# The input norm of a hybrid encoder block: token by token from a token-major copy, instead of raw projections that are scaled afterwards

## The chip, the cores and the metric

The kernel runs on one core of one Trainium2 chip. The metric is the device time of one execution in microseconds (us). The core has five engines that run side by side: PE (TensorE, matmuls; its weight loads are listed as PEld), DVE (VectorE), ACT (ScalarE), POOL (GpSimd) and SP (SyncE, which here only issues transfers). Work passes between them by semaphores.

## The reference, cut to what matters

One layer: an RMS norm, one wide projection `w_in`, three token mixers whose results are gated and merged, an output projection, and an MLP. What the change touches is the first norm and the first users of its result:

```python
def rms_norm(x, g):
    y = x * lax.rsqrt(jnp.mean(x * x, axis=-1, keepdims=True) + EPS)
    return y * g

h = rms_norm(x, norm1_g)                  # x: 512 tokens x 1024 features
p = h @ w_in                              # N_IN = 3*1024 + 2*1024 + 3*1024 + 3*1024+256 columns
pa, pb, pg, pc = _split(p, ...)
pc = token_shift(pc, rwkv_mu)             # p + (previous token's p - p) * mu
r, k, v, xw, xa, xg = _split(pc, ...)     # 1024, 1024, 1024, 64, 64, 128 columns
decay = exp(-exp(-softplus(-(w0 + tanh(xw) @ w2)) - 0.5))
a = sigmoid(a0 + xa @ a2);  g_c = sigmoid(xg) @ g2
# short convolution, RG-LRU, RWKV-7 recurrence over chunks of 64 tokens, merge with gates
x = x + m @ w_out
x = x + square(relu(rms_norm(x, norm2_g) @ mlp_w1)) @ mlp_w2
return rms_norm(x, final_g)
```

All of it is float32. The norm's factor belongs to a token, so it commutes with a projection: `(x * g) @ w` can be formed first and its row multiplied by the token's root afterwards.

## The kernel before, in words

**Layout.** Activations stand feature-major: 128 features on the partitions, the 512 tokens (`S`) along the row, eight such tiles (`KT`) for 1024 features. A projection of 128 columns (a "chunk") takes eight 128x128 weight tiles. To keep float32 accuracy each operand is split into a rounded high half and a remainder, `whi`/`wlo` for a weight and `hh`/`hl` for the normed input, and `mm3` (L168 to L171) issues three matmuls for each tile, so a chunk is 24 matmuls of 128x512. A weight is loaded on SP's queue into one of two `raw` buffers, ACT casts the high half (L148), and DVE subtracts for the low half (L105); three buffers of each half rotate.

**The start.** SP loads x feature-major (`xT`, from `xt`) in five pieces, with halves of the first two weights between them. For each of the eight tiles ACT forms `xgh` (x times the norm's gain, rounded) and the square, DVE the remainder `xgl` and the sum of two squares, and PE adds the squares over the features by a matmul with a tile of ones into `pst`. PE projects from `xgh` and `xgl` at once, before the root is known: chunk `lr 0`, later `lr 1`, `k 0` and `r 0` (`proj_raw`; these are the raw projections). `rsqrt_rows` makes the root on DVE by two transposes and three Newton steps. Then `pro_scale` multiplies `xT` by the root and makes `hh` and `hl`, which all further chunks use, and `unscaled` multiplies the four raw results by the root.

**The order.** A scheduler orders each engine's queue by priority. Generators are woven: `krv(g)` prepares the keys, values and receptance of head group g (`pw`, `pa`, `pn`, `pb`, `pV` are its small matmuls), `amat(g)` the matrices within chunks (`pA`, masked by DVE into `AXt`, then transposes `pB`), `inverse` inverts them, `chain` is the recurrence; the steps of `ab(q)` and `gate(q)`, projections of the other two mixers and of the gates, fill in between. `weave(krv(0), fl, R0)` takes 0.85 fill steps for each step of `krv(0)`. In `krv` the first k and r were not projected, since `k0` and `r0` existed.

**POOL.** It issues the transfers through DRAM that rearrange heads and chunks. `ttd` is a DRAM buffer of which one part is zeroed from a tile `zer`; `in_eyes` is a table of identities for `inverse`, loaded into a tile that shares its buffer (tag Z) with half of `xgh`.

Of the kernel before, what the change touches and what calls it, by code (L numbers as in the profile page):

```python
# [99 lines left out]
def block_kernel(ctx, tc, xt, win, par, mulr, sw, wout, w1, w2, fg, cst, eyes, out):  # L100
# [3 lines left out]
    def tt(o, a, b, op):  # L104
        return v.tensor_tensor(out=o, in0=a, in1=b, op=op)  # L105

    def stt(o, a, s, b, op0, op1):
        return v.scalar_tensor_tensor(out=o, in0=a, scalar=s, in1=b, op0=op0, op1=op1)  # L108
# [59 lines left out]
    def mm3(ps, wh, wl, xh, xl, start=True, stop=True):  # L168
        pe.matmul(ps, wh, xh, start=start, stop=False)  # L169
        pe.matmul(ps, wh, xl, start=False, stop=False)  # L170
        pe.matmul(ps, wl, xh, start=False, stop=stop)  # L171
# [71 lines left out]
    wlr = [new_w()]
    load_half(wlr[0], win[CN[("lr", 0)]], 0)
    for a, n in ((0, 1), (1, 1), (2, 2)):
        sy.dma_start(xT[:, a:a + n], xt[a:a + n].rearrange("k p t -> p k t"))
    load_half(wlr[0], win[CN[("lr", 0)]], 1)
    for a, n in ((4, 2), (6, 2)):
        sy.dma_start(xT[:, a:a + n], xt[a:a + n].rearrange("k p t -> p k t"))
    wlr.append(new_w())  # L250
    for i in range(2):
        load_half(wlr[1], win[CN[("lr", 1)]], i)
    gp.memset(epst[:, 0:1], EPS)
# [1 line left out]
    gp.memset(one, 1.0)
    wu = pc.tile([P, S], F32, tag="pu", name="wu")
    for i in range(NWARM):
        pe.matmul(wu, ones, zer, start=True, stop=True)
    pst = pm.tile([P, S], F32, tag="pm", name="pst")
    warm = pro.tile([P, 1], F32, name="warm")  # L260
    ac.activation(warm, epst[:, 0:1], AF.Tanh)

    t_lr0 = pp.tile([P, S], F32, tag="pp", name="pp")
    sqp_ctx = ExitStack()
    sqp = sqp_ctx.enter_context(tc.tile_pool(name="sqp", bufs=1))
    for kt in range(KT):
        sq = (p1 if kt % 2 else sqp).tile([P, S], F32, tag=f"v{kt // 2 % 2}" if kt % 2 else f"sq{kt // 2}", name="sq")
        ac.activation(xgh(kt), xT[:, kt], AF.Copy, scale=n1t[:, kt:kt + 1])
        stt(xgl[:, kt], xT[:, kt], n1t[:, kt:kt + 1], f(xgh(kt)), MUL, SUB)
        with tc.high_priority(offset=OFFP):  # L270
            ac.activation(sq, xT[:, kt], AF.Square)
            if kt % 2 == 1:
                tt(sq, sq, sq_, ADD)
                pe.matmul(pst, ones, sq, start=kt == 1, stop=kt == KT - 1)
        mm3(t_lr0, *wslice(wlr[0], kt), xgh(kt), xgl[:, kt], start=kt == 0, stop=kt == KT - 1)
        sq_ = sq
# [6 lines left out]
    sy.dma_start(ident, cst[:, 0:P])  # L283
    sy.dma_start(mask, cst[:, 2 * P:3 * P])

    def pro_scale():
        for kt in range(KT):
            tt(xT[:, kt], xT[:, kt], rsb, MUL)
            ac.activation(hh[:, kt], xT[:, kt], AF.Copy, scale=n1t[:, kt:kt + 1])
            stt(hl[:, kt], xT[:, kt], n1t[:, kt:kt + 1], f(hh[:, kt]), MUL, SUB)  # L290
        ac.copy(bd, c0)

    def proj_raw(w, t):
        for kt in range(KT):
            mm3(t, *wslice(w, kt), xgh(kt), xgl[:, kt], start=kt == 0, stop=kt == KT - 1)
# [64 lines left out]
    shift(unscaled(t_lr0, "us0"), mul[:, 0:1], omul[:, 0:1], lr)  # L360
    t_k0 = pp.tile([P, S], F32, tag="pp", name="pp")
    proj_raw(load_w(win[CN[("k", 0)]]), t_k0)
    t_r0 = pc.tile([P, S], F32, tag="pS", name="r0")
    proj_raw(load_w(win[CN[("r", 0)]]), t_r0)
# [57 lines left out]
    def krv(g, G_):  # L422
# [3 lines left out]
        for jj in range(2):  # L426
            j = 2 * g + jj
            if j == 0:
                ks, rs = k0, r0
            else:  # L430
                ks, rs = WP("ks"), WP("rs")
                t = yield from proj(("k", j))
                shift(t, pv("mu_k", j), dvp(OMK, j), ks)
# [882 lines left out]
```

## Time and profile before

| | us |
|---|---|
| median of 3 runs | 1028.8 |
| lowest, highest | 1027.36, 1030.81 |
| the profiled execution | 1029.49 |
| its span on the core | 1027.7 |

| engine | busy us | share of the span |
|---|---|---|
| PE | 1007.2 | 98% |
| PEld | 817.7 | 80% |
| DVE | 735.1 | 72% |
| ACT | 512.9 | 50% |
| POOL | 110.1 | 11% |

The profile is one execution, recorded by the hardware. The span runs from the first instruction of the program to the last; what lies around it is the difference to the execution's time, 1.8 us. A row of the order of time has the start, the length, the engine, the line in the kernel, the operation, what it writes and reads, its shape and how many were merged, and in brackets the idle time of the engine before it and what ended it. PE's matmuls are pipelined: their lengths overlap, so the distance of two starts tells what one costs.

### The profile page before, as it was taken

To read this page: it belongs to the slowest core of one execution; us is meant where nothing else is said; L and a number is where in the kernel's file an instruction comes from. 1 tells how busy PE (TensorE), PEld (TensorE's weight loads), DVE (VectorE), ACT (ScalarE), POOL (GpSimd) and SP (SyncE) were. 2 spreads that over 40 slices of the span, in tenths; PEclk is the share of its full clock that TensorE was granted. 3 is DMA by queue.
4 is the path that set the end of the run, shared out by engine and by line. 5 is a ranking of instruction groups with operands and counts; after the bars stand their busy time and mean duration, and the time that the engine had idled before them with its cause. 6 is when DMAs were issued, how large, how long until landed. Compare 5 with 4: busy or idle time off the path is not lost. (4 is left out here: it accounts for less than half of the span.)

```text
span 1027.7 us, 15699 instructions
## 1 busy us (share of the span) xinstructions
PE 1007.2 (98%) x6110; PEld 817.7 (80%) x6110; DVE 735.1 (72%) x1251; ACT 512.9 (50%) x757; POOL 110.1 (11%) x179
## 2 busy tenths in 40 slices
PE   8999999999999999999999999999999999999997
PEld 5777877888887788888787877888888888878885
DVE  6997497599865886794668779656554546887775
ACT  7756453655554655456446344435433334454344
POOL 1013011201212112001322100100000000000001
PEclk9999999999999999999999999999999999999999
DMA  6444643734546446434897724544333325644442
GB/s 231 129 123 112 185 134 114 215 107 128 150 134 164 136 126 161 158 95 122 268 256 243 220 87 119 174 132 130 90 99 103 98 87 164 226 127 139 143 166 102
DMA packets 49177, 151.53 MB, mean 147 GB/s; under 512 B 6544, under 2 KB 10128, under 8 KB 48080
## 3 DMA queue, kind: packets, MB, share of 16 engines
q1 hardware_dynamic: 34816, 99.93, 30.6%
q0 software_dynamic: 13568, 49.56, 18.0%
q8 instruction: 48, 0.79, 0.3%
q10 hardware_dynamic: 720, 1.05, 0.3%
q14 instruction: 25, 0.20, 0.1%
HBM read 123.78 MB, written 26.74 MB: 146 GB/s over the span
## 5 line engine op out<-in xcount | busy, mean ns | idle before, releaser
L148 ACT CAST whi<-raw 128x1024 fp32r<-128x1024 f32 (+1 forms) x164 | 169.7, 1037 | 257.0 <-PE pp L170 86.7
L105 DVE TENSOR_TENSOR wlo<-raw,whi 128x1024 fp32r<-128x1024 f32 (+1 forms) x176 | 206.5, 1175 | 91.2 <-ACT whi L148 90.6
L169 PE MATMUL pp<-hh,whi 128*128 128x512 f32 x688 | 271.2, 395 | 0.4 <-DVE rs L108 0.4
L170 PE MATMUL pp<-hl,whi 128*128 128x512 f32 x688 | 270.1, 393 | 0.0
L171 PE MATMUL pp<-hh,wlo 128*128 128x512 f32 x688 | 269.1, 391 | 0.2 <-DVE wlo L105 0.2
L169 PEld LDWEIGHTS pp<-hh,whi 128*128 128x128 f32 x688 | 129.1, 188 | 28.9 <-DVE rs L108 0.9
L171 PEld LDWEIGHTS pp<-hh,wlo 128*128 128x128 f32 x688 | 129.2, 188 | 27.5 <-DVE wlo L105 0.6
L170 PEld LDWEIGHTS pp<-hl,whi 128*128 128x128 f32 x688 | 129.2, 188 | 26.3
L169 PE MATMUL p<-h2h,whi 128*128 128x512 f32 x256 | 100.4, 392 | 0.0
L171 PE MATMUL p<-h2h,wlo 128*128 128x512 f32 x256 | 99.7, 389 | 0.0
L170 PE MATMUL p<-h2l,whi 128*128 128x512 f32 x256 | 99.6, 389 | 0.0
L108 DVE SCALAR_TENSOR_TENSOR r<-p,rsb 128x512 f32<-128x512 f32 x32 | 22.0, 691 | 69.3 <-PE p L171 68.8
L171 PEld LDWEIGHTS p<-h2h,wlo 128*128 128x128 f32 x256 | 48.1, 188 | 10.2
L169 PEld LDWEIGHTS p<-h2h,whi 128*128 128x128 f32 x256 | 48.1, 188 | 9.8
L170 PEld LDWEIGHTS p<-h2l,whi 128*128 128x128 f32 x256 | 48.1, 188 | 9.6
L1225 POOL TENSOR_TENSOR x0f<-xr,fgt 128x512 f32<-128x512 f32 x4 | 5.2, 1296 | 310.6 <-DMA raw<-in_w 301.4
L170 PE MATMUL acc<-ml,whi 128*128 128x512 f32 x64 | 25.0, 391 | 0.0
L171 PE MATMUL acc<-mh,wlo 128*128 128x512 f32 x64 | 25.0, 390 | 0.0
L1076 PE MATMUL acc<-whi,a2h 128*128 128x512 f32 x64 | 24.9, 389 | 0.0
L1076 PE MATMUL acc<-whi,a2l 128*128 128x512 f32 x64 | 24.9, 389 | 0.0
L1076 PE MATMUL acc<-wlo,a2h 128*128 128x512 f32 x64 | 24.9, 389 | 0.0
L1076 PE MATMUL acc<-whi,ah 128*128 128x512 f32 x64 | 24.9, 389 | 0.0
(368 smaller groups left out, 1733.5 us busy)
## 6 DMA issues: line engine op xcount, KB each, us to landing
raw<-in_win SPq DMA_DIRECT2D x88, 512.0 KB, 3.6
raw<-in_w SPq DMA_DIRECT2D x64, 512.0 KB, 3.6
ax<-axd POOLq DMA_DIRECT2D x8, 1024.0 KB, 10.0
axd<-AXt POOLq DMA_DIRECT2D x12, 512.0 KB, 8.7
raw<-in_w SPq DMA_DIRECT2D x24, 256.0 KB, 2.9
bkd<-BKT POOLq DMA_DIRECT2D x4, 1024.0 KB, 15.4
raw<-in_wout SPq DMA_DIRECT2D x8, 512.0 KB, 3.6
bk<-bkd POOLq DMA_DIRECT2D x7, 512.0 KB, 13.0
```

The costliest lines, as they stand in the source:

```text
L105: return v.tensor_tensor(out=o, in0=a, in1=b, op=op)
L108: return v.scalar_tensor_tensor(out=o, in0=a, scalar=s, in1=b, op0=op0, op1=op1)
L148: ac.copy(hi[:, sl], raw[:, sl])
L169: pe.matmul(ps, wh, xh, start=start, stop=False)
L170: pe.matmul(ps, wh, xl, start=False, stop=False)
L171: pe.matmul(ps, wl, xh, start=False, stop=stop)
L1076: pe.matmul(b[i], x_[:, ms], w_, start=id(b[i]) not in begun, stop=last and n == 2, skip_group_check=True)
L1225: gp.tensor_tensor(out=o0, in0=x0, in1=fgt[0], op=MUL)
```

## The change

x comes a second time, as `xn`: four tiles of 128 tokens with all 1024 features in the row, loaded into `xs` at the head of SP's queue. The feature-major copy is no longer loaded here. For each token tile ACT squares the row and accumulates it to one number per token, ACT takes a root, DVE corrects its reciprocal by one Newton step, and multiplies an identity by it to a diagonal `dg`. PE multiplies each 128x128 tile of `xs` by the diagonal (`turn`), which transposes it to feature-major and scales each token at once, into PSUM banks `tb`; there are 32 such turns. From `tb` ACT and DVE make `hh` and `hl`. All projections now use these, so `proj_raw`, `pro_scale`, `unscaled`, `xgh`, `xgl` and the matmuls over squares are gone. Both `lr` chunks are projected side by side; `k 0` and `r 0` become ordinary steps of `krv(0)`. Ahead of the first turn stand matmuls of ones with ones that keep PE occupied (`warm`, 12 and three after each of the first three tiles). The zeros for `ttd` come from a small tile made later, and a root taken early on ACT before the end's norm is gone.

```diff
-NWARM = 2
+NWARM, NFILL = 12, 3
...
-    xT = p1.tile([P, KT, S], F32, tag="AXt", name="xT")
-    xgh_ = [p1.tile([P, 4, S], F32R, tag=t, name="xgh") for t in ("BKT", "Z")]
+    xs = p1.tile([P, 4, D], F32, tag="AXt", name="xs")
...
+    ac.dma_start(ident, cst[:, 0:P])
     ac.dma_start(n1t, par[:, PI["n1"]])
+    with tc.high_priority(offset=1000):
+        for i in range(3):
+            sy.dma_start(xs[:, i], xn[i])
+        for h in range(2):
+            sy.dma_start(xs[:, 3, h * S:(h + 1) * S], xn[3, :, h * S:(h + 1) * S])
...
+    def warm(n):
+        for i in range(n):
+            pe.matmul(wu[:, 0:P], ones, ones, start=True, stop=True)
+    warm(NWARM)
...
+    def turn(kt, i):
+        pe.matmul(tb[kt][:, i * P:(i + 1) * P], xs[:, i, kt * P:(kt + 1) * P], dg[:, i], start=True, stop=True)
+
+    with tc.high_priority(offset=1000):
+        for i in range(4):
+            if i < 3:
+                ac.activation(junk, xs[:, i], AF.Square, accum_out=ssq[:, 0, i:i + 1])
+            else:
+                for h in range(2):
+                    ac.activation(junk[:, h * S:(h + 1) * S], xs[:, 3, h * S:(h + 1) * S], AF.Square,
+                                  accum_out=ssq[:, h, 3:4])
+                tt(ssq[:, 0, 3:4], ssq[:, 0, 3:4], ssq[:, 1, 3:4], ADD)
+            ac.activation(ssq[:, 1, i:i + 1], ssq[:, 0, i:i + 1], AF.Sqrt, bias=epst[:, 0:1], scale=1.0 / D)
+            m_, y_ = ssq[:, 0, i:i + 1], ssq[:, 1, i:i + 1]
+            v.reciprocal(y_, y_)
+            ts2(m_, m_, -0.5 / D, -0.5 * EPS, MUL, ADD)
+            stt(m_, m_, y_, y_, MUL, MUL)
+            stt(m_, m_, 1.5, y_, ADD, MUL)
+            v.tensor_scalar(out=dg[:, i], in0=ident, scalar1=ssq[:, 0, i:i + 1], scalar2=None, op0=MUL)
+            if i < 3:
+                for kt in range(5):
+                    turn(kt, i)
+                warm(NFILL)
+
+    wlr = [load_w(win[CN[("lr", i)]]) for i in range(2)]
...
+    def normed(kt):
...
+        for i in range(3 if kt < 5 else 0, 4):
+            turn(kt, i)
+        ac.activation(hh[:, kt], tb[kt], AF.Copy, scale=n1t[:, kt:kt + 1])
+        stt(hl[:, kt], tb[kt], n1t[:, kt:kt + 1], f(hh[:, kt]), MUL, SUB)
...
+        for kt in range(KT):
+            if kt and kt + 4 < KT:
+                normed(kt + 4)
+            for w, t in zip(wlr, t_lr):
+                mm3(t, *wslice(w, kt), hh[:, kt], hl[:, kt], start=kt == 0, stop=kt == KT - 1)
...
-    def pro_scale():
-        for kt in range(KT):
-            tt(xT[:, kt], xT[:, kt], rsb, MUL)
...
-    def unscaled(t, tag):
...
-            if j == 0:
-                ks, rs = k0, r0
-            else:
...
+            ks, rs = WP("ks"), WP("rs")
+            t = yield from proj(("k", j))
...
-        gp.dma_start(ttd[32:64, g, :, 0:32], zer[0:32, 0:32].unsqueeze(1).to_broadcast([32, NC * 4, 32]))
+        gp.dma_start(ttd[32:64, g, :, 0:32], zz.unsqueeze(1).to_broadcast([32, NC * 4, 32]))
...
-        ac.activation(epst, epst, AF.Sqrt)
-        gp.memset(epst, EPS)
```

How the queues change at the places that matter. First PE at the start of the program, before (`wu` is the bank of the warming matmuls, `pst` the sum of squares, `pp` a projection's bank):

```order
L258 MATMUL wu<-zer,ones 128x512 x2
L274 MATMUL pst<-sq,ones 128x512
L169 MATMUL pp<-xgh,whi 128x512
L170 MATMUL pp<-xgl,whi 128x512
L171 MATMUL pp<-xgh,wlo 128x512
L169 MATMUL pp<-xgh,whi 128x512
L274 MATMUL pst<-sq,ones 128x512
```

And PE now, from the last token tile's turns on (`tb_124` to `tb_249` are the eight feature tiles, `pp_200` is lr 0 and `pp_201` lr 1):

```order
L262 MATMUL tb_128<-dg_131,xs_97 128x128
L169 MATMUL pp_200<-hh_73,whi_189 128x512
L170 MATMUL pp_200<-hl_74,whi_189 128x512
L171 MATMUL pp_200<-hh_73,wlo_190 128x512
L262 MATMUL tb_223<-dg_131,xs_97 128x128 x4
L169 MATMUL pp_200<-hh_73,whi_189 128x512
L170 MATMUL pp_200<-hl_74,whi_189 128x512
L171 MATMUL pp_200<-hh_73,wlo_190 128x512
L169 MATMUL pp_200<-hh_73,whi_189 128x512
L169 MATMUL pp_201<-hh_73,whi_195 128x512
```

The first projection, which came behind one matmul over two tiles' squares, now comes behind the turns of all four token tiles. Next ACT at the same place, now:

```order
L270 ACTIVATE junk_129,ssq_130<-xs_97 128x512 x2
L273 ACTIVATE ssq_130<-ssq_130,epst_68 128x1
L148 CAST whi_189<-raw_188 128x1024
L294 ACTIVATE hh_73<-tb_124,n1t_101 128x512
L294 ACTIVATE hh_73<-tb_125,n1t_101 128x512
L294 ACTIVATE hh_73<-tb_126,n1t_101 128x512
L294 ACTIVATE hh_73<-tb_127,n1t_101 128x512
L294 ACTIVATE hh_73<-tb_128,n1t_101 128x512
L148 CAST whi_195<-raw_194 128x1024
L294 ACTIVATE hh_73<-tb_223,n1t_101 128x512
```

The first weight's cast stands ahead of the first `hh`, the second weight's cast between the fifth and the sixth. Last, POOL at the start, before:

```order
L308 MEMSET smk 128x512
L874 DMA ttd<-zer 32x32x32
L309 MEMSET smk 128x8
L874 DMA ttd<-zer 32x32x32 x3
L463 MEMSET PPt 128x8
L1057 MEMSET epst 128x1
L562 DMA Z<-in_eyes 128x1024
L489 DMA rtd<-AR 128x8x64
```

and now:

```order
L323 MEMSET smk 128x512
L555 DMA Z<-in_eyes 128x1024
L324 MEMSET smk 128x8
L482 DMA rtd<-AR 128x8x64
L456 MEMSET PPt 128x8
```

The zeros of `ttd` have left the start, and the load of the identities for `inverse`, whose buffer is no longer held by raw x, has come forward to it.

More of the change, by code (lines that the diff above doesn't have):

```diff
@@ L99, in block_kernel @@
 @with_exitstack
-def block_kernel(ctx, tc, xt, win, par, mulr, sw, wout, w1, w2, fg, cst, eyes, out):
+def block_kernel(ctx, tc, xt, win, par, mulr, sw, wout, w1, w2, fg, cst, eyes, xn, out):
     nc = tc.nc
@@ L239, in block_kernel @@
-    gp.memset(zer, 0.0)
     gp.memset(ones, 1.0)
+    gp.memset(epst[:, 0:1], EPS)
     n1t = pro.tile([P, KT], F32, name="n1t")
+    ac.dma_start(ident, cst[:, 0:P])
     ac.dma_start(n1t, par[:, PI["n1"]])
[L243 to L253, printed above, removed]
+    with tc.high_priority(offset=1000):
[3 more added lines that the diff above has]
+            sy.dma_start(xs[:, 3, h * S:(h + 1) * S], xn[3, :, h * S:(h + 1) * S])
     one = cp.tile([P, 1], F32, name="one")
     gp.memset(one, 1.0)
-    wu = pc.tile([P, S], F32, tag="pu", name="wu")
-    for i in range(NWARM):
-        pe.matmul(wu, ones, zer, start=True, stop=True)
@@ L259, in block_kernel @@
[L259 to L265, printed above, removed]
-    for kt in range(KT):
[L267 to L276, printed above, removed]
@@ L277, in block_kernel @@
-    with tc.high_priority(offset=OFFP):
-        rsqrt_rows(pro, rsb, pst, EPS, 1.0 / D)
+    wu = pp.tile([P, S], F32, tag="pp", name="wu")
+    def warm(n):
+        for i in range(n):
+            pe.matmul(wu[:, 0:P], ones, ones, start=True, stop=True)
+    warm(NWARM)
+    tb = [pc.tile([P, S], F32, tag=t, name="tb") for t in ("pu", "pS", "py")] + \
+        [pm.tile([P, S], F32, tag="pm", name="tb") for _ in range(2)]
+    junk = pro.tile([P, D], F32, name="junk")
+    ssq = pro.tile([P, 2, 4], F32, name="ssq")
@@ new lines, in block_kernel @@
+    dg = pro.tile([P, 4, P], F32, name="dg")
+    root = pro.tile([P, 1], F32, name="root")
+    ac.activation(root, epst[:, 0:1], AF.Sqrt)
+    def turn(kt, i):
[20 more added lines that the diff above has]
+                warm(NFILL)
@@ new lines, in block_kernel @@
+    wlr = [load_w(win[CN[("lr", i)]]) for i in range(2)]
+    t_lr = [pp.tile([P, S], F32, tag="pp", name="pp") for _ in range(2)]
+    def normed(kt):
+        if kt >= 5:
+            tb.append(pm.tile([P, S], F32, tag="pm", name="tb") if kt > 5 else
+                      pc.tile([P, S], F32, tag="pu", name="tb"))
+        for i in range(3 if kt < 5 else 0, 4):
+            turn(kt, i)
+        ac.activation(hh[:, kt], tb[kt], AF.Copy, scale=n1t[:, kt:kt + 1])
+        stt(hl[:, kt], tb[kt], n1t[:, kt:kt + 1], f(hh[:, kt]), MUL, SUB)
@@ L279, in block_kernel @@
+    with tc.high_priority(offset=1000):
+        for kt in range(5):
+            normed(kt)
+        for kt in range(KT):
[3 more added lines that the diff above has]
+                mm3(t, *wslice(w, kt), hh[:, kt], hl[:, kt], start=kt == 0, stop=kt == KT - 1)
     c0 = pro.tile([P, P], F32, name="c0")
@@ L282, in block_kernel @@
     sy.dma_start(c0, cst[:, P:2 * P])
-    sy.dma_start(ident, cst[:, 0:P])
     sy.dma_start(mask, cst[:, 2 * P:3 * P])
-    def pro_scale():
-        for kt in range(KT):
-            tt(xT[:, kt], xT[:, kt], rsb, MUL)
[L289 to L295, printed above, removed]
+    ac.copy(bd, c0)
     mpd = dp.tile([KT, P, S], F32, name="mpd")
@@ L359, in block_kernel @@
     lr = WP("ks")
[L360 to L364, printed above, removed]
+    shift(t_lr[0], mul[:, 0:1], omul[:, 0:1], lr)
+    lg = WP("rs")
+    shift(t_lr[1], mul[:, 1:2], omul[:, 1:2], lg)
     ac.activation(lr[0:64], lr[0:64], AF.Tanh)
@@ L427, in krv @@
             j = 2 * g + jj
[L428 to L433 removed]
+            ks, rs = WP("ks"), WP("rs")
+            t = yield from proj(("k", j))
+            shift(t, pv("mu_k", j), dvp(OMK, j), ks)
             sq = WP("a1")
@@ L437, in krv @@
             yield
-            if j:
-                t = yield from proj(("r", j))
-                shift(t, pv("mu_r", j), dvp(OMR, j), rs)
+            t = yield from proj(("r", j))
+            shift(t, pv("mu_r", j), dvp(OMR, j), rs)
             swh, swl = load_sw(pk, "swa", j, 0, 2)
@@ L1294, in pack @@
     return {k: np.ascontiguousarray(a, dtype=a.dtype) for k, a in z.items()}
-_NAMES = ["xt", "win", "par", "mulr", "sw", "wout", "w1", "w2", "fg", "cst", "eyes"]
+_NAMES = ["xt", "win", "par", "mulr", "sw", "wout", "w1", "w2", "fg", "cst", "eyes", "xn"]
 def kernel(**inputs):
```

21 lines of the change are left out of this document (3 added, 18 removed).

## The prediction

> **What bounds the kernel now.** I read the page first, then the stretches of time, then each engine in order of time over the first 100 us.
>
> ```profile
> PE 1007.2 (98%) x6110; PEld 817.7 (80%) x6110; DVE 735.1 (72%) x1251; ACT 512.9 (50%) x757; POOL 110.1 (11%) x179
> ```
>
> PE is busy for 98% of the span, so the whole is bound by PE: its matmuls at their pitch, plus the gaps in which it waits. The change leaves the number of projection matmuls alone, so only gaps can move. The stretches show where they are (columns: stretch, then busy time and count of PE, weight loads, DVE, ACT and POOL, the granted PE clock, the DMA share and GB/s):
>
> ```profile
> 0.00:5.00 5.00, 3.49 (x4) 1.17 (x4) 0.00 (x0) 3.68 (x6) 3.93 (x13) 1.00 0.57 163
> 5.00:10.00 5.00, 2.43 (x5) 1.30 (x5) 2.40 (x4) 3.49 (x7) 0.79 (x1) 0.79 1.01 340
> 10.00:15.00 5.00, 4.87 (x14) 2.48 (x13) 4.02 (x7) 4.65 (x10) 0.14 (x2) 0.86 1.04 376
> 50.00:60.00 10.00, 9.59 (x43) 7.59 (x41) 9.94 (x28) 5.20 (x9) 0.91 (x1) 1.00 0.42 137
> 60.00:70.00 10.00, 9.98 (x43) 7.95 (x44) 9.53 (x23) 6.71 (x11) 1.50 (x3) 1.00 0.43 112
> 70.00:80.00 10.00, 9.88 (x44) 7.84 (x43) 9.63 (x24) 6.43 (x10) 0.89 (x1) 1.00 0.37 113
> ```
>
> Two things are to be seen. PE does little before 10 us, and DVE is full from 50 to 80 us (9.94, 9.53 and 9.63 of 10). Next, PE in order of time (start, length, instruction, and in brackets the idle time before it and who ended it):
>
> ```profile
> 1.46 3.49 PE L258 MATMUL wu<-zer,ones 128*128 128x512 f32 x4 [1.46 <-POOL one L255]
> 7.57 1.75 PE L274 MATMUL pst<-sq,ones 128*128 128x512 f32 x2 [2.62 <-DVE sq L105]
> 9.54 0.63 PE L170 MATMUL pp<-xgl,whi 128*128 128x512 f32 x1
> 9.97 0.63 PE L171 MATMUL pp<-xgh,wlo 128*128 128x512 f32 x1
> 35.26 0.39 PE L171 MATMUL r<-xgh,wlo 128*128 128x512 f32 x1
> 35.49 0.39 PE L169 MATMUL pp<-hh,whi 128*128 128x512 f32 x1
> 50.58 0.39 PE L169 MATMUL pp<-hh,whi 128*128 128x512 f32 x1
> ```
>
> From 50.58 to the row at 59.20 below PE starts 38 matmuls without a gap: 8.62/38 = 0.227 us is the pitch of one 128x512 matmul. The four raw projections (lr 0, lr 1, k 0, r 0) are 4 x 24 = 96 matmuls, and the 97th starts at 35.49. At full pitch 96 take 21.8 us, so 13.7 us of the first 35.49 went to the start, to the squares (pst) and to waits. This is my reference point: when does the changed kernel start its 97th?
>
> Behind it, PE waits for DVE at four places while the first group of heads is prepared:
>
> ```profile
> 59.20 0.39 PE L171 MATMUL pp<-hh,wlo 128*128 128x512 f32 x1
> 60.02 0.50 PE L169 MATMUL pp<-hh,whi 128*128 128x512 f32 x1 [0.43 <-DVE rs L108]
> 80.31 0.39 PE L171 MATMUL pp<-hh,wlo 128*128 128x512 f32 x1
> 80.98 0.51 PE L499 MATMUL pb<-bl,bd 128*128 128x512 f32 x1 [0.28 <-DVE bl L105]
> 87.68 2.22 PE L529 MATMUL pA<-AR,BK 64*128 64x128 f32 x32
> 91.56 3.02 PE L529 MATMUL pA<-AR,BK 64*128 64x128 f32 x32
> 95.31 0.40 PE L169 MATMUL pp<-hh,whi 128*128 128x512 f32 x1
> 96.54 1.97 PE L551 MATMUL pB<-ident,BK 128*128 128x128 f32 x16 [0.83 <-DVE AXt L105]
> ```
>
> Against the pitch, 59.20 to 60.02 loses 0.6 us and 80.31 to 80.98 loses 0.4; the second block of 32 pA is 0.8 longer than the first; 95.31 to 96.54 loses 1.0. Together 2.8 us.
>
> **The change part by part.**
>
> *x lands.* The rows that show x arriving before, and the work that POOL issues:
>
> ```profile
> 6.17 0.63 ACT L271 ACTIVATE sq<-xT 128x512 f32<-128x512 f32 x1 [1.27 <-DMA xT<-in_xt]
> 11.01 1.15 ACT L271 ACTIVATE sq<-xT 128x512 f32<-128x512 f32 x2 [0.35 <-DMA xT<-in_xt]
> 35.96 0.58 POOL L562 DMA_DIRECT2D Z<-in_eyes  x1 [21.22 <-PE r L171]
> ```
>
> And a stretch in which the queues are full:
>
> ```profile
> 3.00:4.00 1.00, 1.00 (x2) 0.33 (x1) 0.00 (x0) 1.00 (x1) 1.00 (x2) 1.00 1.06 371
> ```
>
> Before, the last of x comes at 11.0 us, since weights are loaded between its pieces. Now the 2.1 MB of x stand alone at the head of SP's queue, with 64 KB of the identity on ACT's. At 371 GB/s (3 to 4 us), with some 0.3 MB moved by 3 us, they are through at 3 + 1.87/0.371 = 8.0 us. Against that, POOL's four small ttd loads leave the start, but Z<-in_eyes (0.5 MB, at 35.96 before because its buffer held raw x) comes forward to it: sharing the same DMA engines it can cost up to 0.52/0.371 = 1.4 us. Bounds 8.0 and 9.4, I take 8.9, nearer the late end because POOL's load would be moving just when the last pieces of x do.
>
> The Trainium skill says so too: DMA: Bandwidth & Descriptors, section Issuing engines are not separate DMA queues, has transfers of all queues interleave on the same 16 engines, which speaks against moving the eyes forward. By a strict half-and-half share the sum would take 9.4 and end 0.5 us later. The trace agrees as far as shares of 1.01 and 1.04 between 5 and 15 us show full engines.
>
> *From the last token tile to its diagonal.* The prices are those of the final norm, which does the same small steps:
>
> ```profile
> 1019.69 0.62 ACT L1224 ACTIVATE fj<-xr 128x512 f32<-128x512 f32 x1
> 1020.21 0.19 ACT L1224 ACTIVATION_READ_ACCUMULATOR fj<-xr 128x1 f32 x1
> 1021.06 0.15 DVE L105 TENSOR_TENSOR fsd<-fss 128x1 f32<-128x1 f32 x1
> 1021.25 0.29 ACT L1229 ACTIVATE fsd<-fsd,epst 128x1 f32<-128x1 f32 x1 [0.85 <-DVE fsd L105]
> 1021.57 0.17 DVE L1230 RECIPROCAL fsd<-fsd 128x1 f32<-128x1 f32 x1 [0.36 <-ACT fsd L1229]
> 1021.77 0.75 DVE L108 SCALAR_TENSOR_TENSOR xr<-xr,fsd,fgt 128x512 f32<-128x512 f32 x1
> ```
>
> Square with its accumulator 0.7 us, then add to root 0.2, root to reciprocal 0.3, and 0.2 for each DVE step that depends on the one before (1021.57 to 1021.77): three more and the diagonal, some 0.9. With hand-offs 2.3 us: the last diagonal is ready at 11.2. The first three tiles' squares (twice 0.62 each) fit in front of it on ACT.
>
> *From there to the stream.* ACT and DVE now set the pace. The page's row of a weight load, and the pieces:
>
> ```profile
> raw<-in_win SPq DMA_DIRECT2D x88, 512.0 KB, 3.6
> ```
>
> ```profile
> 24.76 1.03 ACT L148 CAST whi<-raw 128x1024 fp32r<-128x1024 f32 x1
> 31.26 1.95 ACT L289 ACTIVATE hh<-xT,n1t 128x512 fp32r<-128x512 f32 x3
> 31.72 1.22 DVE L105 TENSOR_TENSOR wlo<-raw,whi 128x1024 fp32r<-128x1024 f32 x1
> 32.86 2.07 DVE L108 SCALAR_TENSOR_TENSOR hl<-xT,n1t,hh 128x512 fp32r<-128x512 f32 x3
> 28.42 1.89 DVE L105 TENSOR_TENSOR xT<-xT,rsb 128x512 f32<-128x512 f32 x3
> ```
>
> One hh is 0.61 us on ACT (three in 1.95), one hl 0.66 on DVE. The two lr weights are loaded behind x (0.5 MB each, 1.4 us: about 10.4 and 11.9), and ACT casts the first of them before any hh. So: cast to 11.6, five hh from 11.7 to 14.9, second cast to 15.9, sixth hh to 16.5, its hl to 17.2, and the second weight's low half on DVE to 18.4. PE's first lr 1 product with that half starts at 18.5; by then 11 of the 48 lr matmuls and 31 of the 32 turns are done. A turn is not in the trace: 32 pA records in 2.22 us make 0.13 for two passes, 16 transposes in 1.97 about 0.11 a pass, so 0.13 to 0.23 each. Either fits in the gaps ahead of 18.5, which hide the turns (31 x 0.23 = 7.1 us at most) so long as 15 of them and the 21 warming matmuls are done while x is still landing. The 18 warming matmuls in front are 36 passes of a quarter of the length that took 3.49/4 = 0.87 us each at the start before: 0.22 each or 7.9 us in all if PE stays as slow as there, 4 us at the transposes' 0.11. From 1.4 us on they end between 5.4 and 9.3; I take about 7, and then the 15 turns follow the diagonals of their tiles with no backlog at 11.2. At 9.3 the 15 turns and three fillers (4.1 us) would run into 13.4 and put 2 us on the start. Behind 18.5 stand 37 lr matmuls, one turn, 24 of k 0, 24 of r 0 and one more: 86 x 0.227 + 0.2 = 19.7, so the 97th ends near 38.2 and starts at 38.0. Weights and hl for these are ready earlier: k 0's weight, called for when the first low half is done (12.9), is 3.6 us under way by the page and has its own low half near 20; the last hl is done near 22. Against 35.49 that is **2.5 us later**; bounds 0.8 (x at 8.0, hand-offs half as long) and 4.
>
> *What DVE no longer does.* Eight xT products at 0.60 (three in 1.89), four "unscaled" copies at 0.60, three of the eight xgl that came after 19 us at 0.66: 9.2 us less on DVE in the stretch in which it was full. The removed squares and root were earlier. PE meanwhile has 30 more fill matmuls (6.8 us) before the first pA: k 0 and r 0 are now steps of the woven generator, which pulls five more fill steps. So DVE has slack at the four places shown. I take all of the first two (1.0 us) and of the other 1.8, where pB waits for four masked products that start only after pA, three quarters: **2.4 us back**; bounds 0.5 and 2.8.
>
> *At nothing.* The ttd writes move behind the first group on POOL's queue, ahead of the transfers of the first pA results; they are read only in the recurrence, far behind. The warming root for the end is gone: a table is loaded again at the end in both orders. The later order shifts by 30 matmuls everywhere; its waits, for instance this one, may come or go, and I put plus or minus 2 us on that:
>
> ```profile
> 143.73 0.39 PE L170 MATMUL pp<-hl,whi 128*128 128x512 f32 x1
> 145.32 0.50 PE L455 MATMUL pn<-bh,bd 128*128 128x512 f32 x1 [1.20 <-ACT a L446]
> ```
>
> *Sum.* Plus 2.5, minus 2.4: 0.1. The profiled execution took 1029.49 us (span 1027.7), 0.7 above the median of 1028.8; on the median's scale **1028.9 us**.
>
> **The rivals.**
>
> *Slower: PE is at half clock when x is there.* After a gap of 2.62 us the matmuls at 9.54 and 9.97 are 0.43 apart, and the clock of 5 to 15 us is 0.79 and 0.86. If the warming matmuls end early and the turns are too sparse, the 11 matmuls and 16 turns before 18.5 (6.2 us at full clock in 7.3 us) take 12.4: 5 us later, 1033.9. It decides when PE stands nearly empty for some 3 us before 11, or when the 18 warming matmuls run past 9. Against it: what stands ahead and five turns per tile fill most of that time. Chance 0.12.
>
> The Trainium skill, TensorE: Matmul & The Clock Gate, section The HAM clock gate, has the clock halve only after a free-running window of about 3.4 us without work; the trace agrees, since 0.79 and 0.86 of two 5 us stretches miss 1.75 us of clock, as 3.5 us at half rate would. By it the new order stays at full clock and the sum stands.
>
> *Nothing is given back.* DVE is full, but PE loses only 2.8 us for it; if the new weave waits elsewhere as much, the later start is all that is left: 1028.8 + 2.5 = 1031.3, and beyond 1031.9 with x at 9.4 and later waits. Chance 0.20, a third of it beyond.
>
> *Faster.* Should x land at 8.0 with brisk hand-offs (plus 0.8), everything be given back (minus 2.8) and the waits at 145.32 (1.4) vanish: 1028.8 - 3.4 = 1025.4. For it: x ahead of the weights on an emptier queue. Against: three favours at once. Chance 0.17.
>
> **How the numbers follow.** The forecast has 0.51, its own range is 1026.4 to 1031.4. 0.3% is 3.1 us (about what can be told from no change), so "same" is 1025.7 to 1031.9. Faster 0.17; slower 0.12 + 0.07 = 0.19; the rest is same. The range from 1025.2 to 1033.0 reaches into both outer cases and leaves out some 0.2.
>
> **What would show it.** The last square near 9 us; first hh product near 12.5; 97th projection matmul near 38; granted clock 1.00 from 8 us on; DVE below 9 of 10 between 50 and 80; gaps before pb and pB under 0.5. Wrong it is if x lands after 10, if the clock falls, or if the later weave gains or loses over 2 us.

## The result: the change makes the kernel 1.3% slower, and the profile after

The changed kernel takes 1043.0 us (median of 4 runs, 1041.91 to 1043.39) where the kernel before took 1029.62 on the same chip: ratio 1.0131, 95% interval 1.0113 to 1.0148. The forecast of 1028.9 us and its range, up to 1033.0, were too low. The profiled execution took 1043.39 us, its span is 1041.5 us, 13.8 more than before. First the page's row of busy times:

```profile
PE 1016.7 (98%) x6204; PEld 832.9 (80%) x6204; DVE 726.0 (70%) x1233; ACT 505.9 (49%) x751; POOL 109.0 (10%) x178
```

DVE lost the 9 us of work that the change takes from it (735.1 to 726.0), and PE is as full as before: a share of 98% hides 13.8 us. The stretches that the prediction showed (columns as there):

```profile
0.00:5.00 5.00, 3.96 (x18) 3.96 (x19) 0.00 (x0) 1.67 (x3) 1.75 (x11) 1.00 0.55 175
5.00:10.00 5.00, 4.66 (x40) 4.46 (x39) 1.76 (x10) 3.66 (x7) 0.00 (x0) 1.00 1.03 407
10.00:15.00 5.00, 3.85 (x29) 3.25 (x28) 3.44 (x13) 4.08 (x11) 0.00 (x0) 1.00 0.70 253
50.00:60.00 10.00, 10.00 (x45) 8.28 (x45) 9.25 (x15) 5.00 (x8) 1.51 (x3) 1.00 0.48 117
60.00:70.00 10.00, 10.00 (x45) 8.26 (x44) 7.43 (x11) 5.97 (x9) 0.00 (x0) 1.00 0.30 75
70.00:80.00 10.00, 10.00 (x46) 8.26 (x44) 9.49 (x23) 4.07 (x6) 2.23 (x3) 1.00 0.42 127
```

From 50 to 80 us PE now has no gap at all, and the clock reads 1.00 at the start. Next PE in order of time at the start:

```profile
1.04 6.32 PE L250 MATMUL wu<-ones 128*128 128x128 f32 x36 [1.04 <-POOL one L245]
13.41 1.38 PE L262 MATMUL tb<-dg,xs 128*128 128x128 f32 x10 [0.37 <-DVE dg L279]
14.67 0.50 PE L169 MATMUL pp<-hh,whi 128*128 128x512 f32 x1
20.43 0.49 PE L171 MATMUL pp<-hh,wlo 128*128 128x512 f32 x1
40.10 0.40 PE L171 MATMUL pp<-hh,wlo 128*128 128x512 f32 x1
```

The last row is the 97th projection matmul: 40.10 against 35.49, so the start costs 4.6 us. ACT's rows tell where it begins:

```profile
5.16 1.06 ACT L267 ACTIVATE junk<-xs 128x1024 f32<-128x1024 f32 x1 [1.80 <-DMA xs<-in_xn]
9.11 1.06 ACT L267 ACTIVATE junk<-xs 128x1024 f32<-128x1024 f32 x1 [1.11 <-DMA xs<-in_xn]
10.49 0.61 ACT L270 ACTIVATE junk<-xs 128x512 f32<-128x512 f32 x1
11.11 0.61 ACT L270 ACTIVATE junk<-xs 128x512 f32<-128x512 f32 x1
13.93 3.00 ACT L294 ACTIVATE hh<-tb,n1t 128x512 fp32r<-128x512 f32 x5 [0.66 <-PE tb L262]
```

The third block of x lands at 9.1 us, and the two half squares of the fourth follow it one behind the other. The rest of the loss comes after 95 us. PE's largest waits there, which the kernel before does not have at this size:

```profile
100.63 0.40 PE L171 MATMUL pp<-hh,wlo 128*128 128x512 f32 x1
102.12 3.64 PE L522 MATMUL pA<-AR,BK 64*128 64x128 f32 x32 [1.09 <-DVE AXt L105]
192.65 0.40 PE L171 MATMUL pp<-hh,wlo 128*128 128x512 f32 x1
194.42 0.76 PE L544 MATMUL pB<-ident,BK 128*128 128x128 f32 x5 [1.38 <-DVE AXt L105]
265.52 0.39 PE L170 MATMUL pp<-hl,whi 128*128 128x512 f32 x1
268.34 0.80 PE L448 MATMUL pn<-bh,bd 128*128 128x512 f32 x1 [2.43 <-ACT a L439]
269.36 0.63 PE L171 MATMUL pp<-hh,wlo 128*128 128x512 f32 x1
269.78 0.63 PE L169 MATMUL pp<-hh,whi 128*128 128x512 f32 x1
```

265.52 to 268.34 loses 2.6 us against the pitch of 0.227. Behind it matmuls start 0.42 apart, half the pace: a second loss, from the clock.

To add such losses up I took, for each pair of successive matmuls on PE, the distance of their starts less 0.227 us behind a 128x512 product (less their own distance, at most 0.11, behind a smaller one), and summed it over stretches. Times in us:

| kernel | 97th starts | excess 25-95 | 95-450 | 450-650 | from 650 | span |
|---|---|---|---|---|---|---|
| before | 35.49 | 4.7 | 11.9 | 12.3 | 2.6 | 1027.7 |
| changed | 40.10 | 1.1 | 25.6 | 10.0 | 3.5 | 1041.5 |

So plus 4.6 at the start, minus 3.6 up to 95 us, plus 13.7 from 95 to 450, minus 1.4 behind: 13.3 of the 13.8. What stands between 95 and 450 are the stages of head groups 0 to 3. Each row of such a table is one execution, the profiled one.

### The profile page after: what moved, and what is told of

Its sections match the earlier page's. It is cut to its first block, busy times and chain, and to the rows that moved or that the text cites. A ratio compares the mean times of both kernels' runs of the same rounds, so it can differ in the third digit from the quotient of the medians.

```text
span 1041.5 us, 15865 instructions
## 1 busy us (share of the span) xinstructions
PE 1016.7 (98%) x6204; PEld 832.9 (80%) x6204; DVE 726.0 (70%) x1233; ACT 505.9 (49%) x751; POOL 109.0 (10%) x178
## 4 chain that ended last, share of the span: by engine, by line
PE 61%; DVE 3%; ACT 2%; DMA 1%; issue 1%; DVEq 0%; ACTq 0%
PE acc L1069 13%; PE pp L169 7%; PE pp L170 7%; PE pp L171 7%; PE p L169 6%; PE p L171 6%; PE p L170 6%; PE acc L171 1%; PE acc L169 1%; PE acc L170 1%; DMA raw<-in_w 1%; PE py L658 1%; PE pu L648 1%; DVE wlo L105 1%; PE pu L668 1%; PE pS L677 1%
## 5 line engine op out<-in xcount | busy, mean ns | idle before, releaser
L148 ACT CAST whi<-raw 128x1024 fp32r<-128x1024 f32 x162 | 169.3, 1048 | 265.3 <-PE pp L170 100.0
L169 PE MATMUL pp<-hh,whi 128*128 128x512 f32 x720 | 284.8, 397 | 1.2 <-DVE v L108 1.2
L170 PE MATMUL pp<-hl,whi 128*128 128x512 f32 x720 | 283.1, 393 | 0.3 <-DVE hl L108 0.3
L171 PE MATMUL pp<-hh,wlo 128*128 128x512 f32 x720 | 282.8, 393 | 0.6 <-DVE wlo L105 0.6
L169 PEld LDWEIGHTS pp<-hh,whi 128*128 128x128 f32 x720 | 135.7, 188 | 30.9 <-DVE v L108 1.6
L171 PEld LDWEIGHTS pp<-hh,wlo 128*128 128x128 f32 x720 | 135.6, 188 | 29.6 <-DVE wlo L105 1.1
L170 PEld LDWEIGHTS pp<-hl,whi 128*128 128x128 f32 x720 | 135.8, 189 | 28.3 <-DVE hl L108 0.6
L1069 PE MATMUL acc<-wlo,ah 128*128 128x512 f32 x64 | 25.0, 391 | 0.4 <-DVE wlo L105 0.4
L1069 PE MATMUL acc<-whi,al 128*128 128x512 f32 x64 | 24.9, 389 | 0.0
```

The costliest lines, as they stand in the source:

```text
L148: ac.copy(hi[:, sl], raw[:, sl])
L1069: pe.matmul(b[i], x_[:, ms], w_, start=id(b[i]) not in begun, stop=last and n == 2, skip_group_check=True)
```

## The experiments

**The theories.** A: the start costs 4.6 us, DVE's relief gives most of it back, and the loss is that the later order is shifted by 30 matmuls, because `k 0` and `r 0` became steps of `krv(0)` and its weave pulled five more fill steps. B: the loss is in the new norm itself, its clock, or the zeros on POOL's queue. The table at the end of this section holds all runs.

**k0 and r0 ahead of the weave.** Inside the changed kernel:

```diff
+    t_k0 = now(proj(("k", 0)))
+    t_r0 = now(proj(("r", 0), pc, "pS"))
...
-            ks, rs = WP("ks"), WP("rs")
-            t = yield from proj(("k", j))
...
+            if j == 0:
+                ks, rs = k0, r0
+            else:
+                ks, rs = WP("ks"), WP("rs")
+                t = yield from proj(("k", j))
...
+            if j:
+                t = yield from proj(("r", j))
```

> The changed kernel, but k0 and r0 are projected (from hh and hl) and shifted in one go ahead of the weave, as the two raw projections stood before; the weave of krv(0) then pulls as many fill steps as before, and from the first pA on the order of the projections is that of the kernel before (first pA after 288 projection matmuls instead of 318). Theory A (about 4.6 us are lost at the start, the other 9 in waits of the order that is shifted by 30 matmuls): 1033 to 1036 us. Rival B (the loss is in the new norm, its clock or the zeros written on POOL's queue, whatever the later order): 1041 to 1045 us.

Measured 1033.15 us, ratio 1.0023 (1.001 to 1.0036). Of the 13 us, ten (11 by the ratios) are gone with the whole new norm still in place, and the waits of the kernel before stand in their old places, 5 us later (before: 95.31, then pB with 0.83 idle at 96.54):

```profile
100.34 0.40 PE L169 MATMUL pp<-hh,whi 128*128 128x512 f32 x1
101.56 1.97 PE L561 MATMUL pB<-ident,BK 128*128 128x128 f32 x16 [0.83 <-DVE AXt L105]
```

**The kernel before with five more fill steps.**

```diff
             if j == 0:
+                for _ in range(3):
+                    yield
                 ks, rs = k0, r0
...
+            if j == 0:
+                for _ in range(3):
+                    yield
```

> The kernel before, with six more empty yields for the first half of krv(0), so that its weave pulls five more fill steps (30 projection matmuls) and the later order has the phase of the changed kernel (first pA after 318). Nothing of the norm is changed. Theory A: 1036 to 1040 us, 7 to 10 above the kernel before. Rival B: 1028 to 1031 us, as before.

Measured 1038.94 us, ratio 1.0074 (1.0052 to 1.0096): the old norm, and 7.6 us slower by the ratio (the spans are 7.5 apart, of which 1.4 lie at the start: there this execution had the half clock from 8.3 to 15.1 us, the kernel before from 7.9 to 11.4). Between 95 and 450 us the kernel before has four gaps of over 0.5 us above the pitch, 4.5 us together; the changed kernel has eleven (13.0 us) and this run twelve (13.9 us), eleven of them the changed kernel's to a few hundredths. Among them is the longest:

```profile
262.99 0.40 PE L170 MATMUL pp<-hl,whi 128*128 128x512 f32 x1
265.83 0.50 PE L460 MATMUL pn<-bh,bd 128*128 128x512 f32 x1 [2.45 <-ACT a L451]
266.40 0.40 PE L171 MATMUL pp<-hh,wlo 128*128 128x512 f32 x1
266.64 0.40 PE L169 MATMUL pp<-hh,whi 128*128 128x512 f32 x1
```

These two runs decide for A: from 95 to 450 us the shift costs 12.0 us with the old norm (23.9 against 11.9) and 12.9 with the new one (25.6 against 12.7). Rival B, that the norm or POOL's queue costs the 13 us whatever the order, falls; what stays with the new norm is the start's 4.6. Over the whole program the two prices differ more, 7.6 and 10 to 11 us.

**One number: a slower weave.** `R0` 0.68 for 0.85 in the changed kernel.

> The changed kernel with one number changed, R0 0.68 for 0.85, so that the weave of krv(0), which has six more yields than before, pulls about as many fill steps as before; k0 and r0 stay in the weave; groups 1 to 3 start at the same projection count as in the kernel before. Theory A: 1033 to 1036 us. Rival C (k0 and r0 inside the weave cost by themselves, whatever follows): 1040 to 1044 us.

Measured 1032.39 us, ratio 1.0009 (0.9991 to 1.0027), a little under the expectation. Groups 1 to 3 stand where they stood before, and PE's idle time in front of all `pn` products shows what that is worth (who ended it, us of PE and its weight loads added, and how often). In the kernel before it is 3.6, 0.2 and 0.2; in the changed kernel:

```profile
  ACT a L439: 8.4, 8
  ACT a L445: 1.9, 2
```

and in this run, with `R0` 0.68:

```profile
  ACT a L439: 3.8, 7
  ACT bh L164: 0.8, 2
  ACT a L445: 0.2, 1
```

The reason can be read from ACT and DVE in front of the long wait. `pn` needs a bank that ACT frees by its tanh of `pw` (L439). In the changed kernel:

```profile
259.12 2.25 DVE L573 STREAM_TRANSPOSE Z<-Z 128x1024 f32<-128x1024 f32 x1
261.84 1.23 DVE L578 STREAM_TRANSPOSE dg<-Z 64x1024 f32<-64x1024 f32 x1
264.11 2.31 DVE L108 SCALAR_TENSOR_TENSOR u<-u,part,u 128x511 f32<-128x511 f32 x3
266.50 0.62 ACT L164 CAST uh<-u 128x512 fp32r<-128x512 f32 x1 [2.54 <-DVE u L108]
267.03 0.68 ACT L340 ACTIVATE rs<-pp,dv 128x512 f32<-128x512 f32 x1
267.61 0.68 ACT L439 ACTIVATE a<-pw,part 128x512 f32<-128x512 f32 x1
```

The fill step that meets this place is the convolution of `ab(q)`. Its three taps on DVE (`u`) stand behind two transposes of the inverse, ACT's cast `uh` waits 2.54 us for them, and the tanh, whose input `pw` was complete by 264, stands behind that cast in ACT's queue. The same cast, after a wait of 3.10 us for DVE, stands ahead of the wait at 378 us in ACT's queue; the other waits were not followed back so far. With `R0` 0.68 another step of `ab(q)` falls there, one that asks nothing of DVE at this moment:

```profile
255.16 1.04 ACT L148 CAST whi<-raw 128x1024 fp32r<-128x1024 f32 x1
256.10 0.69 ACT L340 ACTIVATE rs<-pp,dv 128x512 f32<-128x512 f32 x1
256.68 0.69 ACT L439 ACTIVATE a<-pw,part 128x512 f32<-128x512 f32 x1
```

In PE's order the same is seen as distance: from group 1 on, `pn` stands 12, 14, 13, 6, 12 and 11 projection matmuls behind its `pw` in the kernel before and in this run, and 9, 7, 8, 6, 6 and 8 in the changed one. The distance does not decide alone: the kernel before loses 1.4 us at the distance of 14 (143.73 to 145.32) and nothing at the distance of 6.

**Groups 2 and 3 alone moved back.** `FILL[2]` (31, 13, 5) for (36, 13, 5) in the changed kernel.

> The changed kernel with one number changed, FILL[2] (31, 13, 5) for (36, 13, 5): group 2 starts five fill steps earlier, so that groups 2 and 3 stand at the projection counts of the kernel before (first pw of group 2 after 888, of group 3 after 1188; pn 13, 8, 12 and 11 projection matmuls behind its pw, where the changed kernel has 8, 6, 6 and 8), while the start, group 0 and group 1 stay as changed. Theory A: the waits of groups 2 and 3 (pn at 265.5, pB at 330.2, pn at 377.3, pA at 325.2 and 409.8 us, and the half-clock window after the first) go, those of group 1 stay: 4 to 7 us under the changed kernel, 1036 to 1039 us. Rival (one late group 0 delays everything behind it): within 1.5 us of the changed kernel, 1041.5 to 1044.5 us.

Measured 1040.83 us, ratio 1.0091 (1.0059 to 1.0123): 2.2 us under the changed kernel by the medians, 4.1 by the ratios. The named waits went, with one exception: pB of group 2, which only fell back to its length in the kernel before (from 1.6 to 1.3 us). But the earlier start of group 2 brought a wait of its own:

```profile
258.02 0.39 PE L170 MATMUL pp<-hl,whi 128*128 128x512 f32 x1
260.78 0.50 PE L171 MATMUL pp<-hh,wlo 128*128 128x512 f32 x1 [2.38 <-DVE wlo L105]
```

So less came than the expected 4 to 7 us, though the named waits went: the excess from 250 to 450 us fell from 14.2 to 10.0, not to the 6.3 of before. A single late group that delays all others, the rival, is refuted by the waits that went; the times alone would not refute it.

**The eyes loaded later.** The second half of `xs` lies in the buffer that the eyes load into:

```diff
-    xs = p1.tile([P, 4, D], F32, tag="AXt", name="xs")
+    xs_ = [p1.tile([P, 2, D], F32, tag=t, name="xs") for t in ("AXt", "Z")]
+    xs = lambda i: xs_[i // 2][:, i % 2]
```

> The changed kernel with the second half of xs in the buffer Z, so that the load of in_eyes into Z on POOL's queue cannot start before the last turns have read it (about 15 us). If this half megabyte is what made x land about 2 us later than taken: last square near 8 to 9 us instead of 11.1, 1040 to 1042 us. If x lands at the rate of its own queue: last square near 11, 1042 to 1044 us.

Measured 1039.91 us, ratio 1.0085 (1.0062 to 1.0109). ACT no longer waits for the third block:

```profile
7.93 1.04 ACT L268 ACTIVATE junk<-xs 128x1024 f32<-128x1024 f32 x1
9.30 0.61 ACT L271 ACTIVATE junk<-xs 128x512 f32<-128x512 f32 x1
9.91 0.61 ACT L271 ACTIVATE junk<-xs 128x512 f32<-128x512 f32 x1
38.89 0.40 PE L171 MATMUL pp<-hh,wlo 128*128 128x512 f32 x1
```

The last piece of x lands at 9.2 us instead of 10.4 (issued at 2.6 in both, 6.6 and 7.8 us on the way), and the 97th starts at 38.89: the eyes cost 1.2 us at the start. The rest of the gain (the spans are 3.9 apart) lies behind 450 us, where the excess is 10.8 against 13.5; from 95 to 450 it is the same 25.6. Nothing ties that part to the eyes: runs differ there by as much.

**Both edits, and DVE's share of the squares.** First `R0` 0.68 with the later eyes, then with that also the last block's square on DVE:

```diff
-                for h in range(2):
-                    ac.activation(junk[:, h * S:(h + 1) * S], xs(3)[:, h * S:(h + 1) * S], AF.Square,
-                                  accum_out=ssq[:, h, 3:4])
-                tt(ssq[:, 0, 3:4], ssq[:, 0, 3:4], ssq[:, 1, 3:4], ADD)
+                v.scalar_tensor_tensor(out=junk2, in0=xs(3), scalar=1.0, in1=xs(3), op0=MUL, op1=MUL,
+                                       accum_out=ssq[:, 0, 3:4])
```

> The changed kernel with both edits, R0 0.68 and the second half of xs in the buffer Z (the load of in_eyes comes after the last turns). Theory A: the 97th projection matmul starts at 38.9 us as in the run with the eyes later, the waits after it are those of the run with R0 0.68: 1.2 us under that run, 1030.5 to 1031.8 us. If the 3 us that the later eyes load gave came from anywhere but the start and the half-clock windows: 1029 us or less.

> As the run before it, and the squares of x's last row block are summed by DVE in one instruction instead of by ACT in two. If ACT's chain of squares (5.2 to 10.6 us) sets the last diagonal, it is ready 0.8 to 1.2 us earlier and the first hh product starts near 12.4 us instead of 13.5: 1029.3 to 1031 us. If x's landing sets it: no change.

Measured 1030.85 us, ratio 1.0001 (0.9983 to 1.0018), and 1030.73, ratio 0.9997 (0.998 to 1.0014). The first is as expected. The second gained nothing at the first hh product (13.16 against 13.22). DVE's square stood in front of the third block's diagonal, so the turns of the last two blocks (20 records) started at 10.91 and ran in one piece; in the first run they start at 10.94 too, behind earlier turns and warm-up products. PE's turns bound the start there, not the squares:

```profile
8.98 1.22 DVE L271 SCALAR_TENSOR_TENSOR junk<-xs 128x1024 f32<-128x1024 f32 x1
10.57 0.29 DVE L279 TENSOR_SCALAR dg<-ident,ssq 128x128 f32<-128x128 f32 x1
10.91 2.50 PE L264 MATMUL tb<-dg,xs 128*128 128x128 f32 x20
```

These are the best versions found. Neither beats the kernel before.

**Without warm-up products.** `NWARM, NFILL = 0, 0`, beside the first of the two.

> The changed kernel with R0 0.68 and the eyes later, but without any of the 21 warm-up products. Rival of the half clock: the turns and the first products run at half clock until one window of 3.41 us was busy; by that the 97th projection matmul starts 1 to 2 us later and the run is 1 to 2 us above the one with warm-ups. If PE has slack behind ACT and DVE there (first products wait for hh and hl anyway): within 0.7 us.

Measured 1032.87 us, ratio 1.0017 (0.9997 to 1.0037). The turns take longer (40 records in 6.99 us, 0.17 each, where 20 took 2.50, 0.125 each), and the 97th product starts at 40.45 instead of 38.62:

```profile
7.24 6.99 PE L263 MATMUL tb<-dg,xs 128*128 128x128 f32 x40 [7.24 <-DVE dg L280]
40.45 0.40 PE L171 MATMUL pp<-hh,wlo 128*128 128x512 f32 x1
```

So the warm-up is worth 1.8 us in the trace; the two times are 2.0 apart with intervals that overlap. The prediction's rival of the half clock had its mechanism right, for a kernel without the warm-up products, but its price was 5 us.

**Two more places for the stages.** `R0` 0.60 and 0.62, with both edits of the start and DVE's square.

> As the run with the squares on DVE, but R0 0.60: one fill step fewer again in krv(0), so that every later stage of groups 0 to 3 starts 6 to 12 projection matmuls earlier in the order. Nothing in the norm or the start differs. Theory A (what a group's waits cost depends on where its stages fall in the order): another set of waits at pA, pB, pn and pb, another time, 1027 to 1037 us, and the same start to 0.1 us. Rival B: the time of the other R0 within 0.7 us.

> As the run with the squares on DVE, but R0 0.62: pn stands 12, 11, 12, 6, 12 and 8 projection matmuls behind its pw in groups 1 to 3 (12, 14, 13, 6, 12 and 11 with R0 0.68). By theory A it is no better than with 0.68 where the distance is shorter (the last group, and the second half of group 1), and its time lies at 1029 to 1034 us; a version faster than the kernel before by over 3 us would say that other waits of the order weigh more than these.

Measured 1033.36 us, ratio 1.0014 (0.9997 to 1.0032), and 1030.86, ratio 1.0000 (0.998 to 1.002). The starts agree (97th at 38.2 and 38.6), the set of waits is another each time. The excess from 95 to 450 is 11.7 in both, under the 12.3 with 0.68; in the profiled executions what was gained there was lost in the recurrence (450 to 650). The times do not tell 0.62 from 0.68. My expectation on the shorter distance to `pn` came half true in the trace with 0.62: `pn` of the last group, now 8 behind its `pw`, loses 1.1 us, but that in the second half of group 1, 11 instead of 14 behind, no longer waits at all.

**DVE's work put back.** Fifteen idle additions into the run with `R0` 0.68:

```diff
+    with tc.high_priority(offset=OFFS):
+        for i in range(15):
+            tt(idle, f(hh[:, i % KT]), f(hl[:, i % KT]), ADD)
```

> The run with R0 0.68, with fifteen idle additions of 128x512 on DVE (hh + hl into a tile that nobody reads), about 9 us of DVE work between 20 and 45 us: what the change took away is put back. If DVE's relief gave back 1.3 to 2.4 us up to the first pA (the prediction's fifth step): 1.3 to 2.4 us above the run with R0 0.68, with waits on DVE's tiles coming back before 95 us. If DVE has slack there: within 0.5 us of it.

Measured 1034.57 us, ratio 1.0034 (1.0012 to 1.0057), 2.2 us above by the medians, 2.6 by the ratios (the two ran on different chips). The total is in the expected range, but not its place: by the trace only 0.8 of it lies ahead of 95 us (excess 3.9 against 3.1), with a wait of `pn` that the unloaded run does not have; the rest is in the recurrence's stretch, where runs differ by themselves. DVE's slack there is nearly whole: 10.3 us more of work between 22 and 40 us cost 0.8.

**All runs** (columns as in the table above; the ratio is to the kernel before on the same chip):

| kernel | ratio | 97th | 25-95 | 95-450 | 450-650 | from 650 |
|---|---|---|---|---|---|---|
| changed | 1.0131 | 40.10 | 1.1 | 25.6 | 10.0 | 3.5 |
| k0, r0 first | 1.0023 | 43.34 | 4.7 | 12.7 | 12.1 | 1.2 |
| before, five more | 1.0074 | 36.93 | 2.3 | 23.9 | 9.0 | 2.2 |
| R0 0.68 | 1.0009 | 39.96 | 3.1 | 13.3 | 11.3 | 1.8 |
| groups 2, 3 back | 1.0091 | 40.03 | 1.1 | 20.8 | 12.2 | 3.0 |
| eyes later | 1.0085 | 38.89 | 1.1 | 25.6 | 8.9 | 1.9 |
| R0 0.68, eyes later | 1.0001 | 38.62 | 4.0 | 12.4 | 14.6 | 2.0 |
| the same, DVE square | 0.9997 | 38.27 | 4.1 | 12.3 | 10.6 | 1.9 |
| R0 0.68, eyes, no warm-up | 1.0017 | 40.45 | 4.6 | 13.3 | 11.1 | 3.5 |
| R0 0.60 | 1.0014 | 38.22 | 3.0 | 11.7 | 15.4 | 1.1 |
| R0 0.62 | 1.0000 | 38.64 | 3.3 | 11.7 | 13.4 | 2.2 |
| R0 0.68, DVE loaded | 1.0034 | 39.93 | 3.9 | 13.2 | 13.8 | 2.8 |

(In "k0, r0 first" small products stand among the first 97, so its 97th is not to be compared. "R0 0.68, eyes later" was profiled in an execution of 1035.61 us, 4.8 above its median: its 14.6 from 450 to 650 belongs to that execution. In "k0, r0 first" and "R0 0.68" less than the start's 4.6 us is left in the times, 2.3 and 1.6 by the medians; the stretches behind 450 us make up 1.6 and 1.8 us by the traces, and the rest is open.)

## Why the prediction was wrong, step by step

- **What bounds the kernel**: right. PE is at 98% in both, and all differences are gaps.
- **x lands**: too early. 8.9 us was taken for all of x, bounds 8.0 and 9.4; the third of the four blocks came at 9.1 and the last piece at 10.4, beyond the bound. The eyes, put at up to 1.4 us, cost 1.2; without them x lands at 9.2 and not at 8.0.
- **From the last tile to its diagonal**: 2.3 us was taken and held to some tenths, 11.11 (the start of the last square) to 13.35. What failed is the sentence that the first tiles' squares fit in front on ACT. A block costs ACT 1.38 us (5.16 to 6.54), and even with the eyes away the four follow each other without a gap and end at 10.5, while the last piece is there at 9.2. The last diagonal came at 13.35 instead of 11.2: 1.5 us of that are x's landing, 0.7 the queue on ACT (10.4 to 11.11).
- **From there to the stream**: right in its steps. The first product with lr 1's low half came at 20.43 instead of 18.5, the 97th at 40.10 instead of 38.0: the 2.1 us that were lost at the diagonal, no more. The whole term of the start was 2.5, bounds 0.8 to 4; it measured 4.6.
- **What DVE no longer does**: this term failed too. Up to 95 us the excess is 3.6 lower than before, but the kernel before with five more fill steps, whose DVE does all of the old work, already has 2.4 of that (2.3 against 4.7). What the relief itself is worth shows where two kernels have the same work behind them, at the first `pw` of group 1 (after 402 projection matmuls, with five more fill steps after 432). With `R0` 0.68 it starts at 126.46 us, 4.5 behind the kernel before (121.95), and the 97th was 4.5 behind as well (39.96 against 35.49): nothing came back. In the changed kernel it starts at 133.00, 2.9 behind the kernel before with five more fill steps (130.15), after 3.2 at the 97th (40.10 against 36.93): 0.3 came back. Putting DVE's work back into the run with `R0` 0.68 costs 0.8 there (127.25). 2.4 was taken, bounds 0.5 and 2.8. The waits at 59 and 80 us are gone, but the loss moved to the next ones: the one in front of the second block of pA stands at 100.63 now and is 1.3 us long instead of 0.8.
- **At nothing**: this step failed. "The later order shifts by 30 matmuls everywhere" was seen and given plus or minus 2 us. It is plus 13.7 from 95 to 450 us. Over the whole program, the run that puts the shift into the kernel before gives 7.6 us for it, and the two runs that take it out win back 10 to 13. Eleven waits decide and not one; the longest (268 us) was followed back to a meeting of a stage with the convolution of `ab(q)`, the others were not followed to their ends. The prediction looked at one wait (143.73) and put down about its size for both signs. The kernel before stands at the good end of what was measured: its excess from 95 to 450 is 11.9, nine of the eleven other runs lie higher and two at 11.7.
- **The rivals**: "nothing is given back" came closest, with its mechanism that the new weave waits elsewhere, but its 1031.3 took the loss as large as the gain. The half clock at the start did not come. It came later, behind the waits, where nobody had placed it. The prediction took it that the clock halves only after a window of about 3.4 us without work, and that the trace agrees; but the gap in its own row is 2.62 us, and the 3.5 us that agree are how long the half clock lasted, not the gap ahead of it.

## What to carry to other kernels

A change that adds or removes steps at the head of a woven program shifts everything behind it, and in a kernel that is 98% full the price of that shift can be larger than all that the change does by itself: count the steps that a weave pulls before and after, and look in the new order at the distance from each small product to what must free its bank. When such a change loses, put the old phase back with one number of the weave before judging the change; here that took 13 us of loss to 1 to 2. And price an ACT or DVE chain by what it costs in its queue for each block, since "fits in front" has to hold for all blocks in a row.

## What the runs showed of the hardware

- **The same wait, with and without the half clock.** Behind a gap of 2.4 us in front of `pn` the matmuls start 0.42 us apart for 3 us in the changed kernel and in the run with later eyes, and 0.23 apart in the kernel before with five more fill steps; behind the gap of 2.38 us at 258 in the run with groups 2 and 3 moved back they are 0.23 apart too. The traces tell the two apart. In all thirteen the stretches between two changes of the granted clock are whole multiples of 3.41 us (in the changed kernel 29, 1, 47, 1 and 224 of them), so the clock changes at the borders of windows of 3.41 us that run on by themselves. The windows around the gap follow, with the columns of the table of stretches.

The changed kernel, where one window has 2.26 us without PE (3.41 less 1.15) and the next one the half clock:

```profile
264.76:268.17 3.41, 1.15 (x5) 0.57 (x4) 3.34 (x6) 1.67 (x3) 0.78 (x1) 1.00 0.87 195
268.17:271.58 3.41, 3.24 (x8) 2.60 (x9) 2.62 (x5) 1.66 (x5) 0.00 (x0) 0.50 0.77 237
```

The kernel before with five more fill steps, where a border falls into the gap and the two windows have 0.98 and 1.54 us without PE:

```profile
260.88:264.29 3.41, 2.43 (x10) 1.34 (x8) 3.34 (x5) 0.54 (x2) 1.36 (x2) 1.00 0.95 141
264.29:267.71 3.42, 1.88 (x8) 1.58 (x9) 3.13 (x5) 2.97 (x6) 0.78 (x1) 1.00 0.88 289
```

In the run with later eyes the gap lies in one window (2.44 us), in the run with groups 2 and 3 moved back in two (1.06 and 1.31). Over the thirteen traces, up to 12 us before their ends, each of the seven windows at full clock that had 1.69 us or more without PE work was followed by the half clock, and of those with 1.54 us or less only one: that which ends at 104.33 us in the changed kernel, with 1.30 us, where most of PE's work are `pA` products on 64 of the 128 rows. What sets that one apart is not shown. The Trainium skill, TensorE: Matmul & The Clock Gate, section The HAM clock gate, calls its window of about 3.4 us free-running, with which the multiples of 3.41 us agree. It has the clock halve after at least one idle window, and here about half a window without PE work was enough.
- **Half pace at the start under a clock that reads 1.00.** The 36 passes of the first 18 warm-up products start 0.213 us apart and then 0.112, a factor of 1.9. The step comes at 5.3 us in the changed kernel and at 4.0 in the run with `R0` 0.68, though the stretch from 0 to 5 us reads 1.00. Without warm-up products the turns run at 0.213 from 7.24 us and step to 0.112 at 12.0. In each of the three the step stands where the trace has its first record of the clock (5.34, 4.00 and 12.01 us). Before that record the pitch tells the pace, the clock's column does not.
- **Where runs differ by themselves.** In the recurrence (450 to 650 us) the excess lies between 8.9 and 15.4 us, with PE waiting in front of products that read the chunk loads, `ax` and `rt` (with `R0` 0.60 and 0.62 the longest wait there, 4.0 and 1.7 us, is for ACT's `u`); among the five runs with `R0` 0.68, whose later order is the same, it goes from 10.6 to 14.6. A difference of that size between two single runs can come from there alone.
